# Feature-wise projections that hold weight blocks, a reordered last mixing, and a gather beside the experts

## The chip, the cores and the metric

The kernel runs on one core of a Trainium2 chip. The core has five engines that run their own instruction streams and wait for each other by semaphores: PE (TensorE, matrix products; PEld is its weight load), DVE (VectorE), ACT (ScalarE), POOL (GpSimd) and SP (SyncE, which here only issues transfers). The metric is the device time of one execution in microseconds, lower is better.

## What is computed

Two models stand one behind the other, on 256 tokens of width 1024, in float32. The first has two layers, each a mixer, a cross attention to a memory of 256 tokens, and a gated feed-forward net, each followed by a layer norm:

```python
x = layer_norm(ALPHA * x + mix(x), ...)                 # layer 0: mLSTM + neighbourhood attention; layer 1: differential attention
x = layer_norm(ALPHA * x + memory_cross_attention(x, mem, wq, wkv, wo), ...)
x = layer_norm(ALPHA * x + swiglu(x, w_gu, w_down), ...)  # hidden width 2816
```

The second has two layers on x and on a context xc of 256 tokens. Layer 1 needs of the context only its keys and values:

```python
h = rms_norm_2(x, n1) * (1 + sc1) + sh1                 # hc from xc likewise
a_b, a_c, a_h, b_v, b_g, c_q, c_k, c_v, d_q, d_k, d_v = split_proj(h @ w_in)
y = concat(short_conv(a), conformer_conv(b), window_attention(c), global_attention(d))  # keys of x and of xc
x = x + g1 * (y @ w_out)
h2 = rms_norm_2(x, n2) * (1 + sc2) + sh2
aff = softmax(h2 @ router)                              # 16 experts
gates, idx = top_k(aff.T, 32)                           # each expert takes 32 tokens
x = x + g2 * scatter(gates * (silu(xs @ w_gate) * (xs @ w_up)) @ w_down)   # xs = h2[idx]
```

## The kernel before

**Number format.** A matrix product of the dense layers is made of three products in the format fp32r: activations are split into a high and a low part (`xh`, `xl`), weights too (`wh`, `wl`), and `prod` adds xh·wh, xl·wh and xh·wl in one PSUM bank. Weights come from HBM in units of 1 MB (128 partitions x 2048 numbers) through a ring of buffers. `split` takes 1024 columns of a unit: ACT copies them to `wh`, DVE subtracts to get `wl`. There are two buffers of each.

**Dense layers.** In `dense_unit` (512 output features, tokens on the output's partitions) the activations are the stationary operand and the weights stream, 512 columns per matmul. Where a later step wants features on the partitions (the convolution's input, query and key of the neighbourhood attention, query and memory key of the cross attention, the hidden layer of the feed-forward net), the result is copied to `tk` or `ffh`, transposed on PE 128x128 at a time, and copied out of PSUM again (`acc_to_T`, and in `ffn` the four transposes of `gu`).

**Streams.** "M" is the main stream, x. "F" is a side stream: memory keys and the context, taken in pieces between the units of the main stream. A third runs the modulation of the second model. In the first block the feed-forward net interleaves `gu(j)` and `down(j)` for 11 blocks of 256 hidden features per layer. A scheduler orders each engine's instructions by priority when the program is built.

**Mixing of the second model.** `mixed` projects x: convolution a (`pa`), convolution b (`pb`), in layer 1 then the keys and values of xc (`kv_unit`), those of x, and last the queries (`query_unit`), all with norm and rotation in small DVE steps ended by transposes (`kd`, `tk`). `drip` puts single taps of the convolution (`cvo`, 128x256 multiply-adds on DVE) between other work, at rates given by `DRIP`. Attention (`attend`, with softmax weights `sx_e` that DVE scales by the reciprocal sum) and `out_proj` follow.

**Experts.** `begin` fetches the first units of the expert weights (2 in layer 0, 5 in layer 1). `route` takes x: transposes, router product, softmax (`aff`), 4 rounds of MAX8 and MATCH_REPLACE for the top 32, ranks (`code`). `gather` builds selection matrices `pm` and multiplies them with the normed x, itself split in `zh` and `zl` (the latter on POOL), into `XS`, 8 blocks of features. Then `expert_unit` goes through the units, 4 experts side by side on PE in layer 1 and 2 in layer 0. The ring of buffers is widened for this stage by `rings` that take over the space of tiles that are no longer used; `ORDER` says in which order, and `fetch` takes them cyclically, so a transfer waits for whoever held that space.

## Time and profile before

| | us |
|---|---|
| runs of the kernel before, median of 3 | 2389.7 (2388.44 to 2394.04) |
| the profiled execution | 2386.75 |
| its span in the trace | 2385.0 |
| outside the span | 1.75 |
| PE busy | 2080.6 (87%) |
| DVE busy | 1180.2 (49%) |
| ACT busy | 710.8 (30%) |

Times in the trace count from the start of the span. The stages are, by the lines and tiles that run in them: the first block up to 1035 us (feed-forward net of its first layer from 310 to 520), mixing of layer 0 from 1035 to 1225, out projection, routing and gather to about 1281, its experts to 1715, mixing and out projection of layer 1 to 1903, its routing and gather to 1930, its experts to 2366, and the last norm. Busy times of matmuls overlap each other's ends and are modelled; spacing from start to start is the better measure.

### The profile page before, as it was taken

What the parts mean: (1) busy time and instruction counts of PE and PEld (TensorE: products, weight loads), DVE (VectorE), ACT (ScalarE), POOL (GpSimd) and SP (SyncE); (2) the same over time, 40 slices, a digit from 0 to 9 for tenths busy, and PEclk for the clock granted to TensorE, in tenths of its full rate; (3) what the DMA queues carried; (4) which work ended last, traced back from release to release, by engine and by line L of the source; (5) the groups of instructions that cost most, each with busy time, mean ns of one, the idle gap of its engine ahead of it and who ended that gap; (6) DMA issues with size and microseconds to landing.
All of it is one profiled execution on the core that took longest, in us unless ns stands there. A gap on an engine that the chain in (4) does not pass through costs nothing.

```text
span 2385.0 us, 26936 instructions
## 1 busy us (share of the span) xinstructions
PE 2080.6 (87%) x10408; PEld 1243.2 (52%) x10408; DVE 1180.2 (49%) x2587; ACT 710.8 (30%) x1184; POOL 26.6 (1%) x20
## 2 busy tenths in 40 slices
PE   8999999999989999989898999988887976666665
PEld 5776777776767777767674333322265721010101
DVE  6586575557687697577973222111179621010001
ACT  5444444443455444444432000000053410000000
POOL 0001000000000000000010000000000000000000
PEclk9999999999999999999988999999998987777777
DMA  7745467666544464436437999999963299999997
GB/s 287 256 176 186 166 233 256 245 234 208 176 142 148 137 203 166 158 128 229 152 138 312 421 421 421 421 421 421 421 228 115 90 392 421 422 421 422 421 422 310
DMA packets 93584, 652.68 MB, mean 274 GB/s; under 512 B 10512, under 2 KB 11024, under 8 KB 15760
## 3 DMA queue, kind: packets, MB, share of 16 engines
q1 hardware_dynamic: 93456, 650.96, 70.7%
q8 instruction: 82, 1.34, 0.2%
q14 instruction: 46, 0.38, 0.0%
HBM read 649.87 MB, written 1.05 MB: 273 GB/s over the span
## 4 chain that ended last, share of the span: by engine, by line
PE 55%; DMA 30%; DVE 10%; ACT 3%; issue 1%; SPq 0%; POOL 0%; DVEq 0%; ACTq 0%; POOLq 0%
PE acc L108 33%; DMA ring<-in_w_up_dram 18%; PE ps L108 17%; DMA ring<-in_w_dn_dram 11%; PE ps L111 3%; DVE wl L124 3%; ACT wh L127 1%; DVE cvo L121 1%; PE acc L111 1%; DMA ring<-in_w_ada_dram 1%; ACT xh L127 0%; DVE z L121 0%; DVE rq_tM L118 0%; DMA ring<-in_w_even_dram 0%; DVE tk L124 0%
## 5 line engine op out<-in xcount | busy, mean ns | idle before, releaser
L124 DVE TENSOR_TENSOR wl<-ring,wh 128x1024 fp32r<-128x1024 f32 x346 | 422.9, 1224 | 243.1 <-ACT wh L127 237.3
L108 PE MATMUL acc<-ring,XS 128*64 128x512 f32 (+1 forms) x2048 | 409.2, 697 | 97.1 <-DMA ring<-in_w_up_dram 53.3
L127 ACT ACTIVATE wh<-ring 128x1024 fp32r<-128x1024 f32 x346 | 366.1, 1060 | 423.5 <-PE acc L108 284.9
L108 PEld LDWEIGHTS acc<-ring,XS 128*64 128x64 f32 (+1 forms) x2048 | 96.3, 129 | 395.6 <-issue 151.2
L108 PE MATMUL acc<-wh,xh 128*128 128x512 f32 (+1 forms) x736 | 289.3, 396 | 10.1 <-ACT xh L127 6.0
L108 PE MATMUL acc<-wl,xh 128*128 128x512 f32 (+1 forms) x736 | 286.6, 394 | 7.8 <-DVE wl L124 7.5
L108 PE MATMUL acc<-wh,xl 128*128 128x512 f32 (+1 forms) x736 | 289.2, 393 | 1.7 <-DVE xl L124 1.7
L121 DVE SCALAR_TENSOR_TENSOR mth<-mth,acc 128x512 f32<-128x512 f32 x24 | 16.5, 688 | 466.2 <-ACT mth L133 466.2
L108 PE MATMUL acc<-ring,hTm 128*64 128x512 f32 (+1 forms) x1024 | 206.4, 699 | 45.6 <-DMA ring<-in_w_dn_dram 44.9
L133 ACT ACTIVATE mth<-acc 128x512 f32<-128x512 f32 x24 | 14.3, 597 | 725.3 <-PE acc L108 725.3
L108 PEld LDWEIGHTS acc<-wh,xh 128*128 128x128 f32 x736 | 140.3, 192 | 42.1 <-ACT xh L127 7.9
L108 PEld LDWEIGHTS acc<-wl,xh 128*128 128x128 f32 x736 | 139.0, 190 | 43.1 <-DVE wl L124 14.0
L108 PEld LDWEIGHTS acc<-wh,xl 128*128 128x128 f32 x736 | 140.6, 191 | 33.0 <-DVE xl L124 5.5
L108 PEld LDWEIGHTS acc<-ring,hTm 128*64 128x64 f32 (+1 forms) x1024 | 47.9, 131 | 190.7 <-DMA ring<-in_w_dn_dram 100.3
L108 PE MATMUL ps<-wh,xh 128*128 128x512 f32 x368 | 145.6, 396 | 0.7 <-ACT wh L127 0.7
L108 PE MATMUL ps<-wh,xl 128*128 128x512 f32 x368 | 145.4, 395 | 0.0
L108 PE MATMUL ps<-wl,xh 128*128 128x512 f32 x368 | 145.0, 396 | 0.1
L124 DVE TENSOR_TENSOR my<-acc,gy 128x512 f32<-128x512 f32 x24 | 16.6, 692 | 227.6 <-PE acc L108 227.6
L108 PE MATMUL ps<-my,GT 128*128 128x512 f32 x160 | 82.3, 656 | 19.4 <-DVE my L124 19.4
L121 DVE SCALAR_TENSOR_TENSOR cvo<-pb,cols,cvo 128x256 f32<-128x256 f32 x180 | 82.0, 481 | 0.3
L108 PEld LDWEIGHTS ps<-wh,xh 128*128 128x128 f32 x368 | 69.2, 188 | 18.4 <-ACT wh L127 2.9
L108 PEld LDWEIGHTS ps<-wh,xl 128*128 128x128 f32 x368 | 69.3, 188 | 16.8 <-issue 3.5
(476 smaller groups left out, 2578.3 us busy)
## 6 DMA issues: line engine op xcount, KB each, us to landing
ring<-in_w_gate_dram SPq DMA_DIRECT2D x128, 1024.0 KB, 19.8
ring<-in_w_up_dram SPq DMA_DIRECT2D x128, 1024.0 KB, 19.8
ring<-in_w_dn_dram SPq DMA_DIRECT2D x128, 1024.0 KB, 19.8
ring<-in_w_ada_dram SPq DMA_DIRECT2D x48, 1024.0 KB, 4.9
ring<-in_w_gu_dram SPq DMA_DIRECT2D x44, 1024.0 KB, 4.9
ring<-in_w_in_dram SPq DMA_DIRECT2D x29, 1024.0 KB, 4.9
ring<-in_w_down_dram SPq DMA_DIRECT2D x22, 1024.0 KB, 4.9
ring<-in_w_memkv_dram SPq DMA_DIRECT2D x16, 1024.0 KB, 4.9
```

The source lines that it names most:

```text
L108: self.nc.tensor.matmul(out, lhsT=lhsT, rhs=rhs, start=start, stop=stop)
L111: self.nc.tensor.transpose(out, in_, self.ident)
L121: (eng or self.nc.vector).scalar_tensor_tensor(out, in0, s, in1, op0=op0, op1=op1)
L124: return (eng or self.nc.vector).tensor_tensor(out=out, in0=in0, in1=in1, op=op)
L127: self.nc.scalar.activation(out=out, in_=in_, func=AF.Copy, scale=scale)
L133: self.nc.scalar.activation(out=out, in_=in_, func=func, **kw)
```

## The change

**Feature-wise units.** A new `dense_T` makes 256 output features of a unit with the weight block stationary and the tokens moving: for a block of 128 inputs and 128 features one matmul of 512 columns (`wh`, with xh and xl side by side in one tile `xp`) and one of 256 columns (`wl`, with xh). On the side stream, where xh and xl are separate tiles, it is three matmuls of 256 columns. The bank's two halves are then added by `join`: an ACT copy of one and a DVE add of the other. It replaces product, copy, transposes and copy in `even_mixer`, the memory keys, the cross attention's queries and the feed-forward net. The host lays out the weights for it.

**Last mixing.** `mixed_last` takes layer 1 in another order: convolution b, queries' product, pre-norm of xc, norm and rotation of the queries, then keys and values of x and xc in one pass (`keys`, one load and split of the weights for both), convolution a, attention. Norm and rotation work on all heads at once. Taps drip at 3 and 4 in place of 2 and 6. In the wide attention of both layers every second scaling of `sx_e` goes to ACT.

**Routing and gather.** `route_start` and half of the transposes and of the router product of x (`route_part`) run within `out_proj`. The exponential of `aff` is issued ahead of the scaling of z and its split. `gather` yields after each of its 8 blocks, and the units already fetched are consumed between them. The ring's order changes.

```diff
+    def dense_T(self, X, w, u, accs=None):
+        accs = accs or [self.acc(), self.acc()]
+        s = self.load(w[u])
+        for q in range(2):
+            wh, wl = self.split(s[:, q * 1024:(q + 1) * 1024])
+            for kk in range(4):
+                k = q * 4 + kk
+                for c in range(2):
+                    ws = slice(kk * 256 + c * 128, kk * 256 + c * 128 + 128)
+                    o = accs[c][:, :256]
+                    if len(X) > 2:
+                        self.mm(accs[c].rearrange("p (a n) -> p a n", a=2), wh[:, ws], X[2][:, :, k], k == 0, False)
+                    else:
+                        self.mm(o, wh[:, ws], X[0][:, k], k == 0, False)
+                        self.mm(o, wh[:, ws], X[1][:, k], False, False)
+                    self.mm(o, wl[:, ws], X[0][:, k], False, k == 7)
...
+    def join(self, dst, acc, two, scale=1.0):
...
+        self.cp(dst, acc[:, 256:], scale)
+        if scale == 1.0:
+            self.tt(dst, acc[:, :256], dst, OP.add)
...
         def gu(j):
-            accs = self.dense_unit(X, self.a["w_gu"][l], j, accs=[self.ps(), self.ps()])
-            h = self.t([128, 2, 256], "ffh")
-            for t in range(2):
...
+            for c in range(2):
+                accs = self.dense_T(X, self.a["w_gu"][l], j * 2 + c, accs=[self.ps(), self.ps()])
+                g, u = self.t([128, 256], "ffg"), self.t([128, 256], "ffu")
+                self.join(g, accs[0], True)
+                self.join(u, accs[1], True)
                 th = self.t([128, 256], "th")
...
+                self.hl(H, c, 1, th[:, None], 0.5)
...
+    def mixed_last(self, x, xc):
+        l = 1
+        X = self.pre(x, l, 0)
+        pa = self.t([128, 2, 258], "pa")
+        self.proj_b(X, l, 0, pa)
+        accs = self.dense_unit(X, self.a["w_in"][l], 1)
...
+        Xc = self.pre(xc, l, 1)
+        self.queries(qs, l)
+        self.keys(X, Xc, l)
+        self.proj_a(X, l, pa)
+        self.begin(l)
...
+                    if self.wide and j:
+                        self.act(e[:, t], e[:, t], AF.Copy, scale=r[:, j, t:t + 1])
+                    else:
+                        self.ts(e[:, t], e[:, t], r[:, j, t:t + 1], None, OP.mult)
...
-        self.act(aff, aff, AF.Exp)
+        self.expd = self.act(aff, aff, AF.Exp)
+        with self.tc.issue_after(self.expd.ins):
+            for t in range(2):
+                self.act(z[:, t], x[:, t], AF.Copy, scale=rs[:, t:t + 1])
...
+        for k in self.gather(z, l, 0, XS):
+            while self.ahead and k > (steps[0][0] + 1) * (4 // ne) - 1:
+                self.expert_unit(*steps.pop(0), ne, part(0))
...
-ORDER = (0, 6, 2, 1, 5, 3, 4), (0, 8, 2, 1, 5, 4, 6, 7, 3)
+ORDER = ((0,), (3, 4), (6, 2, 1, 5)), ((0,), (3, 7), (8, 2, 1, 5, 4, 6))
...
-DRIP = ((2, 6), (1, 0))
+DRIP = ((2, 6), (1, 0), (3, 4))
```

How the instructions move is shown at three places. First, ACT in the feed-forward net of the first block, before: `th` is the tanh of the gate, `hTh` the high part of the transposed hidden block, `adae` belongs to the modulation.

```order
L127 ACTIVATE wh<-ring 128x1024 x2
L133 ACTIVATE th<-ps 128x256
L127 ACTIVATE wh<-ring 128x1024
L133 ACTIVATE th<-ps 128x256
L127 ACTIVATE wh<-ring 128x1024
L127 ACTIVATE hTh<-ps 128x512
```

The same engine and net in the changed kernel; `ffg` and `ffu` are the joined gate and up halves.

```order
L128 ACTIVATE wh<-ring 128x1024
L128 ACTIVATE ffg<-ps 128x256
L128 ACTIVATE wh<-ring 128x1024
L128 ACTIVATE ffu<-ps 128x256
L134 ACTIVATE th<-ffg 128x256
L128 ACTIVATE wh<-ring 128x1024
L128 ACTIVATE hTh<-th 128x256
```

For 128 hidden features there is now one `wh` ahead of each join's copy, and `th` waits for DVE's add in place of PE.

Second, PE in the mixing of layer 1, before, where the last projections of x end (`kd` are keys, `tk` queries, `KT` and `QT` the transposed ones, whose product opens attention).

```order
L108 MATMUL acc<-wl,xh 128x512
L111 MATMUL ps<-tabs,kd 128x128 x8
L111 MATMUL ps<-tabs,tk 128x128 x4
L108 MATMUL acc<-KT,QT 128x256
L111 MATMUL ps<-tabs,tk 128x128 x2
L108 MATMUL ps<-tabs,mods_3431 128x128 x3
L111 MATMUL ps<-tabs,tk 128x128 x2
```

In the changed kernel the queries' transposes stand within the product of the keys:

```order
L109 MATMUL acc<-wh,xh 128x512
L112 MATMUL ps<-tabs,tk 128x128 x4
L109 MATMUL acc<-wh,xl 128x512
L109 MATMUL acc<-wl,xh 128x512
L109 MATMUL acc<-wh,xh 128x512
```

and those of the keys, of both streams, stand behind the 48 matmuls of convolution a:

```order
L109 MATMUL acc<-wl,xh 128x512
L112 MATMUL ps<-tabs,kd 128x128 x16
L112 MATMUL ps<-tabs,cva 128x128 x4
L109 MATMUL ps<-tabs,mods_3722 128x128 x8
L109 MATMUL acc<-KT,QT 128x256 x4
```

So the queries' transposes have moved from the front of attention to a place with dense products ahead and behind; the keys' have stayed in front of attention.

Third, SP at the start of the experts of layer 1, before: each row is a unit of 1 MB, and what it waits for is who held its buffer.

```order
L1266 DMA ring_14291<-in_w_up_dram 128x2048 [waits DMAHW2_49,PE_49]
L1266 DMA ring_14315<-in_w_up_dram 128x2048 [waits DMAHW3_49]
L1266 DMA ring_14333<-in_w_gate_dram 128x2048 [waits DVE_49,DMAHW4_49,PE_49,Activation_49]
L1266 DMA ring_14339<-in_w_up_dram 128x2048 [waits DMAHW5_49,DVE_49,Pool_49]
L1266 DMA ring_14345<-in_w_gate_dram 128x2048 [waits DMAHW6_49,PE_49]
L1266 DMA ring_14351<-in_w_up_dram 128x2048 [waits DMAHW7_49,PE_49]
```

The same place in the changed kernel:

```order
L1425 DMA ring_14998<-in_w_up_dram 128x2048 [waits DMAHW0_49,PE_49]
L1425 DMA ring_15052<-in_w_gate_dram 128x2048 [waits DMAHW1_49,PE_49]
L1425 DMA ring_15058<-in_w_up_dram 128x2048 [waits DMAHW2_49,PE_49]
L1425 DMA ring_15022<-in_w_up_dram 128x2048 [waits DMAHW3_49]
L1425 DMA ring_15040<-in_w_gate_dram 128x2048 [waits DMAHW4_49,DVE_49,Activation_49]
L1425 DMA ring_15046<-in_w_up_dram 128x2048 [waits DMAHW5_49,Pool_49]
L1425 DMA ring_15064<-in_w_gate_dram 128x2048 [waits DMAHW6_49,PE_49]
```

Two units (15052 and 15058), which go into buffers that the first consumed units set free, have moved ahead of three (15022, 15040 and 15046) whose buffers come free with the routing.

## Rows read from the trace of the kernel before

**Rows 1.** The page, part 4: chain that ended last, share of the span

```profile
PE 55%; DMA 30%; DVE 10%; ACT 3%; issue 1%; SPq 0%; POOL 0%; DVEq 0%; ACTq 0%; POOLq 0%
```

**Rows 2.** Windows: length, busy PE, PEld, DVE, ACT, POOL (instructions), clock, DMA share, GB/s

```profile
0.00:1035.00 1035.00, 993.26 (x5107) 762.30 (x5108) 705.42 (x1359) 483.48 (x779) 11.36 (x12) 0.99 0.57 198
310.00:520.00 210.00, 209.17 (x1132) 160.20 (x1130) 121.15 (x183) 93.29 (x123) 0.00 (x0) 1.00 0.68 245
...
1312.00:1715.00 403.00, 367.32 (x1568) 123.36 (x1568) 79.72 (x156) 18.25 (x31) 0.00 (x0) 1.00 1.01 421
1715.00:1903.00 188.00, 155.97 (x763) 113.01 (x760) 141.28 (x391) 77.73 (x143) 0.00 (x0) 0.90 0.43 158
...
1930.00:2366.00 436.00, 297.21 (x1611) 54.04 (x1613) 31.61 (x62) 12.97 (x23) 0.00 (x0) 0.75 1.01 419
```

**Rows 3.** Timeline of PE, matmuls of 512 columns: start, duration

```profile
559.75 0.39 PE L108 MATMUL acc<-wh,xh 128*128 128x512 f32 x1
...
561.79 0.39 PE L108 MATMUL acc<-wh,xh 128*128 128x512 f32 x1
```

**Rows 4.** Timeline of PE, matmuls of 256 columns

```profile
823.68 0.28 PE L108 MATMUL acc<-wh,xl 128*128 128x256 f32 x1
...
825.59 0.28 PE L108 MATMUL acc<-wl,xh 128*128 128x256 f32 x1
```

**Rows 5.** Timeline of PE, four transposes in a row

```profile
332.59 0.60 PE L111 MATMUL acc<-tabs,tk 128*128 128x128 f32 x4
```

**Rows 6.** Waits of PE, first block: waited for, us in total, times, longest

```profile
PE acc L111 <- ACT tk L127: 1.8, 2, 0.9
```

**Rows 7.** Groups of ACT, 310 to 520 us: busy, mean ns, idle before, releaser

```profile
L127 ACT ACTIVATE wh<-ring 128x1024 fp32r<-128x1024 f32 x65 | 68.8, 1060 | 78.8 <-PE ps L108 55.2 <-PE acc L108 22.3
L133 ACT ACTIVATE th<-ps 128x256 f32<-128x256 f32 x22 | 8.2, 374 | 13.3 <-PE ps L108 13.3
```

**Rows 8.** Groups of DVE, 310 to 520 us

```profile
L124 DVE TENSOR_TENSOR wl<-ring,wh 128x1024 fp32r<-128x1024 f32 x66 | 80.8, 1226 | 69.9 <-ACT wh L127 69.8
L124 DVE TENSOR_TENSOR ffh<-th,ps 128x256 f32<-128x256 f32 x21 | 8.8, 420 | 0.6
```

**Rows 9.** Waits of PE, mixing of layer 1

```profile
PE ps L111 <- DVE tk L124: 9.8, 2, 9.5
...
PE ps L111 <- DVE kd L130: 3.2, 4, 1.0
PE ps L111 <- DVE cva L121: 2.7, 2, 2.1
PE acc L111 <- DVE sx_e L116: 2.6, 2, 2.1
```

**Rows 10.** Timeline of all engines, routing of layer 1 to its first units

```profile
1908.97 1.15 ACT L133 ACTIVATE z<-x,rq_zM 128x1024 f32<-128x1024 f32 x1 [2.86 <-DVE rq_zM L118]
...
1910.97 0.21 ACT L133 ACTIVATE aff<-aff 128x32 f32<-128x32 f32 x1
...
1911.14 4.64 POOL L124 TENSOR_TENSOR zl<-z,zh 128x1024 fp32r<-128x1024 f32 x2 [642.86 <-ACT zh L127]
...
1911.64 1.89 DVE L124 TENSOR_TENSOR aff<-aff,rt_rM 128x32 f32<-128x32 f32 x1
...
1915.80 0.33 SPq L1266 DMA_DIRECT2D ring<-in_w_up_dram  x1
...
1921.55 0.77 PE L108 MATMUL acc<-pm,zh 128*128 128x512 f32 x1 [1.10 <-DVE pm L124]
...
1930.43 0.33 SPq L1266 DMA_DIRECT2D ring<-in_w_gate_dram  x1
```

**Rows 11.** Timeline of all engines, routing of layer 0

```profile
1254.49 0.18 DVE L124 TENSOR_TENSOR aff<-rt_qM,rt_mM 128x32 f32<-128x32 f32 x1
...
1260.33 0.21 ACT L133 ACTIVATE aff<-aff 128x32 f32<-128x32 f32 x1
...
1271.12 0.77 PE L108 MATMUL acc<-pm,zh 128*128 128x512 f32 x1 [1.10 <-DVE pm L124]
```

More of the change, by code (lines that the diff above doesn't have):

```diff
@@ L1 @@
+import contextlib
 import itertools
@@ L420, in even_mixer @@
             nc.vector.memset(cpad[u][:, :, 258:260], 0.0)
[L421 to L425 removed]
+        w = a["w_evenT"]
+        for u in range(4):
+            accs = self.dense_T(X, w, u)
+            for c in range(2):
+                self.join(cpad[u // 2][:, (u % 2) * 2 + c, 2:258], accs[c], True)
         gT = self.t([16, 256], "gT")
@@ L652, in cross @@
         qT = self.big([128, 8, 256], "qk")
-        for u in range(2):
-            accs = self.dense_unit(X, self.a["w_memq"][l], u)
-            for t in range(2):
-                self.acc_to_T(accs[t], t, qT[:, u * 4:u * 4 + 4, t * 128:(t + 1) * 128])
+        for u in range(4):
+            accs = self.dense_T(X, self.a["w_memq"][l], u)
+            for c in range(2):
+                self.join(qT[:, u * 2 + c], accs[c], True)
         O = self.pair(8, "x")
@@ new lines, in mixed_last @@
+    def mixed_last(self, x, xc):
[4 more added lines that the diff above has]
+        accs = self.dense_unit(X, self.a["w_in"][l], 1)
+        qs = self.t([128, 2, 512], "qs")
+        for t in range(2):
+            self.cp(qs[:, t], accs[t])
+        Xc = self.pre(xc, l, 1)
[3 more added lines that the diff above has]
+        self.begin(l)
+        g = self.gate_rows(l, 2, 0)
+        self.wide = True
+        for _ in self.attend(l, 0):
+            pass
+        self.wide = False
+        self.convs(l, 0)
+        self.route_start(l, 0)
+        for _ in self.out_proj(l, 0, x, g):
+            pass
@@ L1209, in gather @@
         for t in range(2):
-            parts.append(self.split(z[:, t], self.nc.gpsimd, to and [v[:, t] for v in to]))
+            with (self.tc.issue_after(self.expd.ins) if r == 0 else contextlib.nullcontext()):
+                parts.append(self.split(z[:, t], self.nc.gpsimd, to and [v[:, t] for v in to]))
         for t in range(2):
@@ L1291, in moe, with part @@
         if nr > 1:
-            self.gather(self.zc, l, 1, XS)
-        self.gather(z, l, 0, XS)
+            for _ in self.gather(self.zc, l, 1, XS):
+                pass
+        first = [self.acc(), self.acc()]
+        steps = [(u, p) for u in range(2 * ne) for p in first]
+        def part(g):
+            return lambda k, j: XS[k][:, (g * ne + j) * M:(g * ne + j + 1) * M]
+        for k in self.gather(z, l, 0, XS):
+            while self.ahead and k > (steps[0][0] + 1) * (4 // ne) - 1:
+                self.expert_unit(*steps.pop(0), ne, part(0))
         nc8 = core[0][1]["C8"]
@@ L1302, in moe @@
             self.rings.append((p.__enter__(), n))
-        self.rings = [self.rings[i] for i in ORDER[l]]
-        a = self.a
+        early, late, rest = ([self.rings[i][0] for i in o for _ in range(self.rings[i][1])] for o in ORDER[l])
+        self.turns = itertools.chain(rest, itertools.cycle(early + late + rest))
         for g in range(ng):
@@ L1307, in moe @@
             for f in range(2):
-                pg, pu = self.acc(), self.acc()
-                for u in range(2 * ne):
-                    for p in (pg, pu):
-                        self.expert_unit(u, ne, p, lambda k, j: XS[k][:, (g * ne + j) * M:(g * ne + j + 1) * M])
+                pg, pu = first if g == 0 and f == 0 else (self.acc(), self.acc())
+                if g or f:
+                    steps = [(u, p) for u in range(2 * ne) for p in (pg, pu)]
+                for u, p in steps:
+                    self.expert_unit(u, p, ne, part(g))
                 th = self.t([128, 512], "mth")
```

231 lines of the change are left out of this document (156 added, 75 removed).

## The prediction

> **What bounds the kernel now.** I read the chain of what ended last first: PE holds 55% of it, transfers 30%, DVE 10% [rows 1]. That is an average over stages with different limits, so the windows come next [rows 2]. The first block fills 1035 us and PE is busy for 993 of them, in its first feed-forward net for 209.2 of 210. In both expert stages the DMA engines are busy all the time and move 420 GB/s, while PE keeps up at 1.2 GHz for much of the second one (granted clock 0.75). The mixing of layer 1 lies between: PE is busy for 156 of 188 us, DVE for 141, and neither fills it. So a us of PE work in the first block is worth a us; in the mixing only waits are; in the expert stages only the moment at which the stream of units starts and whether it pauses. The stages follow one another, so gains ahead of an expert stage shift all of it.
>
> **First block: the arithmetic on PE.** Matmuls of 512 columns start 2.04 us / 9 = 0.227 us apart [rows 3], those of 256 columns 1.91 / 16 = 0.119 [rows 4]. A matmul pair of `dense_T` costs 0.346; it does the work of one and a half 512-column products, 0.340. Counted in both programs, 960 pairs replace 1440 products on the main stream: 332.2 against 326.5, +5.7. On the side stream 128 triples of 256 columns replace 192 products: 45.8 against 43.5, +2.3. Away go 184 transposes (88 of `ffh`, 96 of `tk`) at about 0.11 us each, as four in a row span 0.60 of which a single one's latency is 0.27 [rows 5]: −20.2. Sum −12.2. There are two weight loads where there were one and a half; their cost lies inside the measured spacing at either width, since 256-column matmuls of the same kind already run at 0.119 with a load each. The waits of PE for `tk` [rows 6] go with the transposes: −1.8. I take −14.
>
> A page speaks against this edit: the Trainium skill, "TensorE: Matmul & The Clock Gate", section Back-to-back issue gap, gives a sustained spacing of 131 ns for 512 columns and 81 ns for 128, so fewer columns per load cost more per column. An estimate between its two figures is 98 ns for 256, and a pair would cost 229 ns against 196, +32 us over 960 pairs. The trace disagrees with both of its figures: 227 and 119 ns, a ratio of 1.9 [rows 3, 4].
>
> **First block: the joins.** Each of 60 main-stream units (44 in the nets, 8 in the even mixer, 8 in the cross attentions) has two joins: two ACT copies of 128x256 at 0.37 [rows 7] and two DVE adds at 0.42 [rows 8]. In exchange the copies around the transposes go. What hides them: between two `wh` copies ACT sits idle for PE's buffers, 78.8 us over 65 copies, 1.2 each [rows 7], and DVE idles 69.9 us ahead of 66 `wl` [rows 8]. The order on ACT puts one `wh` ahead of each join's copy, so half a unit's split (1.06 + 1.23 = 2.29) stands against 8 × 0.346 = 2.77 us of matmuls, and 0.48 is left: enough for one copy or add in front of it, not for both. I take nothing, with +10 as the other end (0.17 per unit), and −4 more if small stalls around the tails go. Bounds of the first block: −18 to −4.
>
> **Mixing of layer 0.** Half of the `sx_e` scalings leave DVE, each about half a us, in a stage bound mostly by PE: −1, from −4 to 0.
>
> **Routing of layer 0.** `aff` is ready at 1254.67, its exponential runs at 1260.33 behind `XS` copies and the scaling of z, and gather starts at 1271.12 [rows 11]. After, the exponential still stands behind four `XS` copies of the context's gather, but half of the router's product and transposes has gone into the out projection, and z and its split come later. If it issued at once, 5.7 + about 2 would be won; I take −4, from −8 to −1. Experts that start inside the gather only use PE time that the transfers leave.
>
> **Mixing of layer 1.** PE waits 9.8 us for the queries' `tk`, 3.2 for the keys' `kd`, 2.7 for convolution a, 2.6 for `sx_e` [rows 9]. After, the queries' norm and rotation run beside the keys' 96 matmuls (96 × 0.227 = 21.8 us): the 9.8 go. The keys' own chain of both streams now ends the projections: behind the last key matmul come copies, square, reduction, about ten small steps, eight multiplications, the rotation, 16 transposes and copies, with three `wl` (1.23 each) and a dozen taps between them on DVE, some 17 to 18 us from the chain of the same kind in the old trace. Beside it run 48 matmuls of convolution a, 10.9 us. So about 5 to 7 us of wait stay in front of attention. One pass for both streams saves four splits, −5 us of DVE, which is the engine behind most waits here, and two units of transfer. Sum of what goes: 9.8 + 3.2 + 2.7 + 2.6 + some 3 of smaller waits = 21; comes back: 6. I take −15; ends −20 (the chain hidden whole) and −5 (DVE behind in the keys too).
>
> **Routing and experts of layer 1.** The exponential at 1910.97 stood behind z (1.15) and one `zh` on ACT, and the next multiplication took 1.89 us while POOL made `zl` [rows 10]. Both delays go: 1.4 + 1.7. `zl` now runs later, beside the ranks, and may hold up a step there for as long again, so the ends are 1.4 and 5 with the router's half; I take gather 3 us earlier against the out projection. That DVE waits beside POOL agrees with the Trainium skill, "GPSIMD Engine Reference", section Key points: the two contend where DVE has two SBUF inputs.
> On SP the gain is lost again. Before, 18 units were issued by 1915.80, and the next at 1930.43 as the gather ended [rows 10]. After, two units that wait for the first consumed buffers stand ahead of three of the 18, so 15 are issued until the first expert units have run, which I put 4.3 us into the gather. Then 177 units remain in place of 174, at 436 us / 175 = 2.49 each [rows 2]: end = start + 4.3 + 2 + 441 = start + 447, before start + 444. Net 0, from −3 to +5.
>
> **Sum.** −14 −1 −4 −15 + 0 = −34 against the profiled 2386.75: 2353. That run lies 3 us below the median of those shown, 2389.7; from the median it is 2356. I say 2355. All good ends give −53, all bad ones −5; taken as independent the ends spread by about 12, so the likeliest case has its own range of 2340 to 2371.
>
> **Rivals.**
> *Joins eat the first block.* If the copies and adds delay each unit's split by 0.25 us, 15 us come back: 2371. For it: only 0.48 us of each 2.77 is free. Against: ACT's idle time above.
> *Slower.* The place is DVE in the feed-forward nets and mixers: if the in-order engine takes both adds (0.84) ahead of the next `wl` in every unit, PE, which has two weight buffers, stalls for all of it: 60 × 0.84 = +50, 2406. It decides from 34 / 60 = 0.57 us per unit on; slower by 0.3% needs 0.69. For it: DVE is the engine with the least room, 121 us of 210 plus 1.8 per 16 us. Against: the order alternates `wl` and adds.
> *The keys' chain replaces the queries'.* The wait before attention goes from 9.8 to some 15, the mixing wins 2, and the SP order costs its 5: −14 −1 −4 −2 + 5 = −16, 2374.
> *No change.* What PE saves is given back by waits of the same stage for transfers, whose share in the first block is 0.57 [rows 2], and the rest cancels: 2390. Against: a share of 0.57 leaves room.
>
> **Chances.** The forecast 0.64, joins eat it 0.13, keys' chain 0.10, no change 0.05, slower 0.08. Other runs of this kernel spread by 0.2%, so 0.3% (7 us) is about what can be told from no change. Faster takes the first three, 0.87; same 0.05; slower 0.08. The range takes in the likeliest case, most of the second and half of the third: 2338 to 2374.
>
> **What would show it.** In the profile after: no `ffh`, PE spacing 0.346 per pair and no wait of PE for `wl` above a few us in the first block, which ends near 1021; no 9.8 us wait for `tk` in layer 1, but one of 5 to 7 for `kd`; out projection of layer 1 done about 34 us earlier than 1903; gather 3 us closer to it; a pause of DMA in front of the first expert units of layer 1, and an end 447 behind the gather's start. Wrong it would be by waits for `wl` in every unit, or by a longer wait for `kd`.

## The result and the profile after

The changed kernel takes 2359.07 us (median of four runs, 2357.39 to 2359.95) against 2389.07 us beside it on the same chip: a ratio of 0.9884, 95% interval 0.9869 to 0.9899. The forecast was 2355, range 2338 to 2374. The profiled execution took 2359.95 us, its span is 2358.2.

The page of the changed kernel, busy times and the chain that ended last:

```profile
PE 2063.0 (87%) x10896; PEld 1262.1 (54%) x10896; DVE 1188.0 (50%) x2616; ACT 752.4 (32%) x1342; POOL 27.5 (1%) x20
...
PE 55%; DMA 30%; DVE 10%; ACT 3%; issue 1%; POOL 0%; SPq 0%; DVEq 0%; ACTq 0%; POOLq 0%
```

PE lost 18 us of busy time, ACT gained 42, and the chain is that of [rows 1]: averages over the span don't say where 27 us of it went. Three stretches of [rows 2] where they now lie, the third from the first product of gather to the last `hTm` matmul:

```profile
300.50:510.50 210.00, 208.63 (x1309) 168.85 (x1308) 135.70 (x234) 107.24 (x182) 0.00 (x0) 1.00 0.70 250
...
1697.00:1875.50 178.50, 155.19 (x778) 113.78 (x774) 129.03 (x334) 84.81 (x160) 0.00 (x0) 0.94 0.41 154
1891.40:2343.40 452.00, 307.48 (x1652) 60.47 (x1652) 35.58 (x70) 15.30 (x26) 0.00 (x0) 0.75 0.99 413
```

The feed-forward net is still full on PE, with more work on DVE (135.7 of 210, before 121.2) and ACT (107.2, before 93.3). The mixing of layer 1 has 12 us less DVE work. The last stretch of [rows 2] began 8.5 us into the gather. Cut like the line above, the experts of layer 1 in the kernel before read:

```profile
1921.50:2370.10 448.60, 308.37 (x1652) 61.02 (x1652) 35.60 (x70) 15.30 (x26) 0.00 (x0) 0.75 0.99 413
```

So the transfers' share is 0.99 in both: the kernel before had a pause of its own there, at the end of its gather (shares of 0.55 and 0.70 from 1925 to 1935).

For an account by stage I cut both timelines at the same instructions. A stage of the first block ends with the last statistics (`lnst`) of its layer norm; the mixing of the second model is cut at the first product KT·QT and at the last add into x; routing ends with the first product of gather, the experts with the last matmul on `hTm`. By this cut the first block of before ends at 1058.5 us, not at 1035.

| stage, us | before | after | difference | forecast |
|---|---|---|---|---|
| even mixer, first cross attention | 306.9 | 297.4 | −9.5 | |
| first feed-forward net | 229.6 | 226.9 | −2.7 | |
| odd mixer | 178.7 | 172.4 | −6.3 | |
| second cross attention | 93.9 | 98.6 | +4.7 | |
| second feed-forward net | 249.4 | 252.6 | +3.2 | |
| first block together | 1058.5 | 1047.9 | −10.6 | −14 |
| layer 0: mixing | 186.5 | 181.0 | −5.5 | −1 |
| layer 0: routing | 26.2 | 23.9 | −2.3 | −4 |
| layer 0: experts | 461.1 | 460.9 | −0.2 | 0 |
| layer 1: projections | 103.2 | 90.5 | −12.7 | |
| layer 1: attention, out projection | 67.9 | 71.4 | +3.5 | |
| layer 1: mixing together | 171.1 | 161.9 | −9.2 | −15 |
| layer 1: routing | 18.2 | 15.9 | −2.3 | −3 |
| layer 1: experts | 448.5 | 451.9 | +3.4 | +3 |
| sum | 2370.1 | 2343.4 | −26.7 | −34 |

**First block.** What PE waits for there, in us in total, times, longest:

```profile
PE acc L109 <- DVE qk L125: 4.5, 1, 4.5
PE acc L109 <- ACT wh L128: 3.8, 3, 2.3
PE acc L109 <- DVE wl L125: 2.6, 5, 0.8
...
PE acc L112 <- ACT cvb L128: 2.0, 1, 2.0
```

The waits for `tk` [rows 6] are gone. In their place stands one large wait, for a joined query tile `qk`, and small ones for the splits. The timeline around the large one, in the second cross attention, PE, DVE and ACT:

```profile
717.89 0.40 PE L109 MATMUL acc<-xp,wh 128*128 128x512 f32 x1
...
718.95 0.40 PE L109 MATMUL acc<-xp,wh 128*128 128x512 f32 x1
...
719.19 0.28 PE L109 MATMUL acc<-xp,wl 128*128 128x256 f32 x1
...
721.77 1.22 DVE L125 TENSOR_TENSOR x<-z,lnbc 128x1024 f32<-128x1024 f32 x1
...
723.02 0.66 ACT L128 ACTIVATE qk<-acc 128x256 f32<-128x256 f32 x2 [2.57 <-DVE x L125]
...
724.01 0.73 PE L109 MATMUL acc<-xp,wh 128*128 128x512 f32 x1 [4.54 <-DVE qk L125]
```

Three pairs of the new form take 1.06 us, 0.353 each, which the forecast put at 0.346. Then PE starts no matmul from 719.19 to 724.01. The join's copy on ACT was released by DVE's residual update, which reads `z`: the query tile takes the space of `z`, so the join waits for the last reader of `z`, and PE for the banks that the join holds.

In the second feed-forward net, 3.2 us longer, PE waits for `cvb` at its start, the context's convolution input. From one matmul's start to the next it is 2.40 us:

```profile
806.58 0.40 PE L109 MATMUL acc<-wl,xh 128*128 128x512 f32 x1
808.98 0.44 PE L112 MATMUL acc<-tabs,cvb 128*128 128x128 f32 x2 [2.00 <-ACT cvb L128]
```

The same gap is in the kernel before:

```profile
822.80 0.93 PE L111 MATMUL acc<-tabs,cvb 128*128 128x128 f32 x4 [2.00 <-ACT cvb L127]
```

What differs is the granted clock behind it. Windows of PE over the 8 us that begin with the gap (length, busy, clock, DMA share, GB/s), changed kernel, then the kernel before:

```profile
806.70:814.70 8.00, 5.95 (x36) 0.79 0.26 72
```

```profile
820.50:828.50 8.00, 5.95 (x43) 1.00 0.22 76
```

**Feed-forward nets.** Groups of ACT, then of DVE, in the stretch that answers to [rows 7, 8]:

```profile
L128 ACT ACTIVATE wh<-ring 128x1024 fp32r<-128x1024 f32 x65 | 68.7, 1059 | 52.3 <-PE ps L109 24.5 <-issue 14.0 <-PE acc L109 12.8
...
L128 ACT ACTIVATE ffg<-ps 128x256 f32<-128x256 f32 x22 | 8.5, 384 | 35.7 <-PE ps L109 35.7
```

```profile
L125 DVE TENSOR_TENSOR ffg<-ps,ffg 128x256 f32<-128x256 f32 x22 | 9.3, 424 | 16.2 <-ACT ffg L128 16.2
```

The joins cost what similar rows of before said (384 and 424 ns; 374 and 420 were taken). ACT still idles 52 us ahead of `wh`, most of it for PE's buffers: in the first net the joins fit.

**Mixing of layer 1.** Waits of PE:

```profile
PE acc L109 <- ACT xh L128: 4.6, 2, 3.2
PE ps L112 <- ACT kd L128: 3.9, 1, 3.9
PE acc L112 <- DVE sx_e L117: 2.5, 1, 2.5
```

The 9.8 us for the queries' `tk` [rows 9] are gone, and the keys take 3.9, less than the 5 to 7 forecast. New is the wait of 3.2 for `xh`: the out projection's first input comes from `cva`, convolution a. Its taps on DVE in the kernel before and in the changed one (min/median/max in ns, first and last start in us):

```profile
L121 DVE SCALAR_TENSOR_TENSOR cva<-pa,cols,cva x4: 480/480/482, 1771.7 to 1772.9; 128x256 f32<-128x256 f32 x4
```

```profile
L122 DVE SCALAR_TENSOR_TENSOR cva<-pa,cols,cva x4: 474/480/485, 1831.4 to 1835.5; 128x256 f32<-128x256 f32 x4
```

Before, they ran ahead of those of convolution b (`cvo`, from 1782.4 to 1855.3 us); now they run behind them (1748.9 to 1814.8). The change also moved the first multiplication of convolution a into the drip, behind the taps of b.

In attention and out projection together PE waits longer and is busy for less than before:

| attention, out projection of layer 1 | us | PE busy | PE idle | clock |
|---|---|---|---|---|
| kernel before | 67.9 | 62.1 | 5.8 | 0.90 |
| changed kernel | 71.4 | 60.4 | 10.9 | 0.95 |

**Routing and first units of layer 1**, timeline of ACT, DVE, POOL, PE and SP:

```profile
1877.38 1.28 SPq L1425 DMA_DIRECT2D ring<-in_w_up_dram  x2
...
1880.56 0.23 ACT L134 ACTIVATE aff<-aff 128x32 f32<-128x32 f32 x1 [3.46 <-DVE aff L125]
...
1880.70 2.17 ACT L134 ACTIVATE z<-x,rq_zM 128x1024 f32<-128x1024 f32 x2
...
1881.24 0.19 DVE L125 TENSOR_TENSOR aff<-aff,rt_rM 128x32 f32<-128x32 f32 x1
...
1883.89 4.64 POOL L125 TENSOR_TENSOR zl<-z,zh 128x1024 fp32r<-128x1024 f32 x2 [631.81 <-ACT zh L128]
...
1886.48 2.19 DVE L117 TENSOR_SCALAR tk<-tk 16x256 f32<-16x256 f32 x1
...
1891.44 0.76 PE L109 MATMUL acc<-pm,zh 128*128 128x512 f32 x1 [1.10 <-DVE pm L125]
...
1896.14 0.33 SPq L1425 DMA_DIRECT2D ring<-in_w_gate_dram  x1
```

The exponential no longer stands behind z, and the multiplication takes 0.19 where it took 1.89 [rows 10]. The delay beside POOL has moved to the ranks: a TENSOR_SCALAR of 16x256 takes 2.19 us. The same instruction in the kernel before, where POOL was done by then:

```profile
1918.50 0.28 DVE L116 TENSOR_SCALAR tk<-tk 16x256 f32<-16x256 f32 x1
```

SP issues nothing from 1878.7 until 1896.14, 4.7 us into the gather, and the transfers run dry (all engines, windows):

```profile
1890.00:1895.00 5.00, 3.90 (x10) 2.70 (x10) 3.11 (x8) 0.00 (x0) 0.00 (x0) 0.52 0.61 254
1895.00:1900.00 5.00, 5.00 (x38) 1.67 (x38) 0.81 (x1) 0.78 (x1) 0.00 (x0) 1.00 0.57 188
```

Shares of 0.61 and 0.57 over ten us are 4 us without transfers, about as long as the pause of before.

### The profile page after: what moved, and what is told of

Its sections match the earlier page's. It is cut to its first block, busy times and chain, and to the rows that moved or that the text cites. A ratio compares the mean times of both kernels' runs of the same rounds, so it can differ in the third digit from the quotient of the medians.

```text
span 2358.2 us, 28075 instructions
## 1 busy us (share of the span) xinstructions
PE 2063.0 (87%) x10896; PEld 1262.1 (54%) x10896; DVE 1188.0 (50%) x2616; ACT 752.4 (32%) x1342; POOL 27.5 (1%) x20
## 3 DMA queue, kind: packets, MB, share of 16 engines
q1 hardware_dynamic: 93168, 648.86, 71.2%
## 4 chain that ended last, share of the span: by engine, by line
PE 55%; DMA 30%; DVE 10%; ACT 3%; issue 1%; POOL 0%; SPq 0%; DVEq 0%; ACTq 0%; POOLq 0%
PE acc L109 35%; DMA ring<-in_w_up_dram 17%; PE ps L109 16%; DMA ring<-in_w_dn_dram 11%; PE ps L112 3%; DVE wl L125 2%; DVE cvo L122 1%; ACT wh L128 1%; PE acc L112 1%; DMA ring<-in_w_ada_dram 1%; ACT sx_e L134 1%; DMA nab<-in_rpb_dram 1%; ACT xp L128 0%; DVE tk L125 0%; ACT tov L134 0%
## 5 line engine op out<-in xcount | busy, mean ns | idle before, releaser
L109 PE MATMUL ps<-xp,wh 128*128 128x512 f32 x704 | 251.8, 399 | 3.5 <-ACT wh L128 1.9
L109 PE MATMUL ps<-xp,wl 128*128 128x256 f32 x704 | 198.8, 286 | 1.5 <-DVE wl L125 1.5
L109 PE MATMUL acc<-wh,xp 128*128 128x512 f32 x544 | 171.8, 397 | 2.8 <-ACT xp L128 1.6
L109 PEld LDWEIGHTS ps<-xp,wh 128*128 128x128 f32 x704 | 131.5, 188 | 38.1 <-ACT wh L128 5.1
L109 PEld LDWEIGHTS ps<-xp,wl 128*128 128x128 f32 x704 | 132.2, 189 | 11.4 <-issue 6.8
L109 PE MATMUL acc<-wh,xh 128*128 128x512 f32 (+1 forms) x336 | 131.1, 393 | 6.8 <-ACT xh L128 6.8
L109 PE MATMUL acc<-wl,xh 128*128 128x512 f32 (+1 forms) x336 | 129.0, 390 | 6.3 <-DVE wl L125 6.1
L109 PE MATMUL acc<-wh,xl 128*128 128x512 f32 (+1 forms) x336 | 130.7, 389 | 0.6 <-DVE xl L125 0.6
L109 PEld LDWEIGHTS acc<-wh,xp 128*128 128x128 f32 x544 | 101.8, 190 | 27.2 <-ACT wh L128 3.3
L109 PE MATMUL acc<-wl,xp 128*128 128x512 f32 x272 | 107.9, 403 | 0.6 <-DVE wl L125 0.5
```

What stands on the lines that cost most here:

```text
L109: self.nc.tensor.matmul(out, lhsT=lhsT, rhs=rhs, start=start, stop=stop)
```

## The experiments

All start from the changed kernel. Each ratio is against the kernel before on the same chip; the changed kernel's is 0.9884. Where a part of the kernel is concerned, the stage lengths of the table above are compared, each from one profiled execution. The interval of every single edit but one, the old order of the last mixing, overlaps that of the changed kernel, so whole runs alone don't tell them from it. Where an edit doesn't touch them the stages repeat within 1.7 us, with three exceptions: even mixer with first cross attention (294.1 to 297.4), odd mixer (171.2 to 175.8), and attention with out projection of layer 1 (71.2 to 75.1). The last two go with the granted clock: the odd mixer took 171.2 at 1.00 and 175.7 at 0.96; attention and out projection took 71.2 to 71.4 at 0.95 and 74.0 to 75.1 at 0.89 to 0.91, with the same waits of PE.

**Order on SP.** The two units that wait for consumed buffers go behind the three for the routing's buffers.

```diff
         t = next(self.turns).tile([128, UNIT], F32, name="ring")
-        self.nc.sync.dma_start(out=t, in_=next(self.units))
+        n = len(self.issued)
+        with (self.tc.issue_after(self.issued[17]) if ne == 4 and n in (18, 19) else contextlib.nullcontext()):
+            self.issued.append(self.nc.sync.dma_start(out=t, in_=next(self.units)).ins)
```

> The changed kernel, but in layer 1 the two units that wait for the first consumed buffers are issued behind the three whose buffers come free with the routing. Theory (the queue's order idles the transfers): in the changed kernel the DMA engines stand still for about 4 us of 1890 to 1900 us. With the three units ahead there is work for them until the first consumed buffer is free, so the experts end 4 us earlier against the gather's start (448 instead of 452 us from it to the last down product), and the kernel takes 2355 against 2359. Rival (the three buffers come free too late): the two units then queue behind a later wait, and it is the same or 1 to 3 us slower, 2359 to 2362.

2354.26 us (2351.19 to 2356.1), ratio 0.9868 [0.9851, 0.9886]. The experts of layer 1 take 446.1 instead of 451.9, and the transfers don't pause:

```profile
1890.00:1895.00 5.00, 5.00 (x26) 2.41 (x24) 0.81 (x1) 0.78 (x1) 0.00 (x0) 0.80 1.01 418
1895.00:1900.00 5.00, 5.00 (x34) 1.95 (x33) 0.81 (x1) 0.78 (x1) 0.00 (x0) 1.00 1.01 421
```

The order of two rows on SP costs 5.8 us. The theory had 4, and the rival's later wait didn't come.

**Gather alone.** Expert units wait for the whole gather.

```diff
         for k in self.gather(z, l, 0, XS):
-            while self.ahead and k > (steps[0][0] + 1) * (4 // ne) - 1:
-                self.expert_unit(*steps.pop(0), ne, part(0))
+            pass
```

> The changed kernel with gather run to its end before the first expert unit, in both layers; in this build the queue has the two units that wait for consumed buffers behind the three that come free with the routing. Theory (it is the queue's order that costs, and starting inside the gather is worth 3 us): from the gather's start to the last down product layer 1 takes 448 to 449 us as before the change, against 452 changed and 446 with the order mended; the kernel 2356. Rival (units inside the gather are what lengthens it, order apart): 444, 2352.

2360.6 us (2357.33 to 2362.83), ratio 0.9889 [0.9874, 0.9904]. The experts of layer 0 take 464.1 (+3.2). Those of layer 1 take 449.1, 2.8 less than in the changed kernel: in this build SP's rows stand in the good order. Against the run above, which has that order too, it is 3.0 more. So starting experts inside the gather is worth 3 us in each layer; in layer 1 the order that comes with it takes 5.8.

**Deferred updates.** The residual updates, spread over the splits after a layer norm, go in the order mult, mult, add, add, so that `z` is read out earlier. (The change itself had already made eight updates of 512 columns behind two empty places into four of 1024 behind one, which "The change" doesn't list.)

```diff
-        for t in range(2):
-            for j, (src, op) in enumerate(((z, OP.mult), (x, OP.add))):
+        for j, (src, op) in enumerate(((z, OP.mult), (x, OP.add))):
+            for t in range(2):
                 self.lazy.append(...)
```

> The changed kernel, but the postponed updates of x after each layer norm run in the order multiply, multiply, add, add over the two halves of the tokens, so that the tile z, whose space the cross attention's queries take, is read for the last time one weight split earlier. Theory (the join of the queries waits for that tile while it holds the accumulators): the 4.8 us gap of PE at 719 us of the changed kernel shrinks by about 3 us, 2356. Rival (the gap is the load of DVE itself at that place, with the context's work): it stays within 1 us of 4.8, 2359.

2357.32 us (2349.88 to 2358.85), ratio 0.9872 [0.9847, 0.9897]. PE's gap falls from 4.82 to 3.18, where about 3 less was expected, the second cross attention from 98.6 to 96.5: the mechanism holds, the size was half.

For the next run the updates also start one split earlier:

```diff
-        self.lazy += [None]
```

> The changed kernel with the deferred residual updates ordered mult, mult, add, add, as before, and with the empty place in front of them left out, so that each runs one split earlier. In the earlier version without that second step PE's gap behind the first query unit of the second cross attention was 3.18 us (4.82 in the changed kernel). Theory (the query tile shares the space of z and waits for the last reader of z): the gap shrinks by the length of one more split, 2.8 us, to below 1, and the second cross attention falls from 96.5 to 94 or less, the level of the kernel before. Rival (DVE is late there whatever the order, since updates and splits queue on it): the gap stays at 3 and only moves.

2350.74 us (2347.47 to 2359.56), ratio 0.9864 [0.984, 0.9888]. The gap is 1.40, above the 1 expected; the stage is 93.0, below the 93.9 of the kernel before. Of its 5.6 us 3.4 are the gap. The rest goes with the clock: its mean over the stage is 0.97 in the changed kernel, 0.98 in the run above and 1.00 here. PE around the gap:

```profile
716.08 0.28 PE L109 MATMUL acc<-xp,wl 128*128 128x256 f32 x1
717.48 0.50 PE L109 MATMUL acc<-xp,wh 128*128 128x512 f32 x1 [1.12 <-DVE qk L125]
```

In this run the second net takes 250.4, 2.2 less, with the wait for `cvb` as long as ever (2.39). Behind it the clock stays up:

```profile
799.00:807.00 8.00, 5.96 (x46) 1.00 0.30 92
```

PE's busy time in the net falls from 240.8 to 239.2: by that the clock behind the gap is worth 1.6 us.

**The gap at the second net.** The context's two copies `cvb` go ahead of the layer norm's later pieces on ACT.

```diff
             k = self.t([128, 512], "cvb")
-            self.cp(k, accs[t])
+            with (self.tc.high_priority(offset=200) if self.S == "F" else contextlib.nullcontext()):
+                self.cp(k, accs[t])
```

> The changed kernel with the two ACT copies of the context's convolution input (cvb) put ahead of the later pieces of the layer norm's transposed output, at the start of the second feed-forward net. In the changed kernel PE waits 2.40 us for them, and behind the gap the granted clock is 0.79 over 8 us; in the kernel before the same gap of 2.39 us leaves it at 1.00. Theory (the 3 us that the second net lost is that gap's clock, and not its products): without the gap the clock stays at 1.00 over 806 to 822, and the second net falls from 252.6 to 249 or 250, 2 to 3 us of the whole. Rival (the clock fell for another reason, or the net's own products are slower): 252 stays, or only the gap's 2 us or less come back with the clock still low. The late pieces come 1.2 us later on ACT; if PE then waits for them instead, that shows as a wait for xp.

2353.58 us (2351.3 to 2359.89), ratio 0.9868 [0.985, 0.9886]. The second net takes 249.5, 3.1 less, the level of before. The same stretch of PE in this run:

```profile
806.00:814.00 8.00, 7.45 (x54) 1.00 0.24 70
```

PE's idle time of 2.0 us in the gap shrinks to 0.5 and the clock stays up. The 3.1 holds both, half each: 1.5 of lowered clock (PE busy 240.8, now 239.3) and 1.6 of waiting, which the kernel before had too. The theory wanted 249 to 250 and has it. The rival's slower products are out: PE's busy time is below the 241.1 of the kernel before.

**Feed-forward nets in the old form**, weights streaming and hidden blocks transposed, all else as changed.

```diff
-            for c in range(2):
-                accs = self.dense_T(X, self.a["w_gu"][l], j * 2 + c, accs=[self.ps(), self.ps()])
...
+            accs = self.dense_unit(X, self.a["w_gu"][l], j, accs=[self.ps(), self.ps()])
```

> The changed kernel with the feed-forward nets as before (512 features a unit, tokens on the partitions, transposes). Theory from the two traces: the first net takes 208.4 us changed and 211.4 before, the second 226.4 and 224.7, so the feature-wise form is worth 1 us in all, 2360, since in the second net, beside the context's work on DVE, the joins give back what PE saves. Rival (the prediction's sum, 2.7 us saved in either net, and the second net is longer for another reason): 2364.

2362.04 us (2361.15 to 2364.22), ratio 0.9904 [0.9887, 0.992]. The first net takes 231.9 (+5.0), the second 252.5 (−0.1). That fits neither the theory (1 us in all) nor the rival (2.7 in either net). PE in both nets, by windows cut at the same places:

| net | kernel | us | PE busy | PE idle | clock |
|---|---|---|---|---|---|
| first | before | 229.6 | 228.8 | 0.8 | 1.00 |
| first | changed | 226.9 | 225.5 | 1.4 | 1.00 |
| first | old form put back | 231.9 | 228.3 | 3.6 | 1.00 |
| second | before | 249.4 | 241.1 | 8.3 | 1.00 |
| second | changed | 252.6 | 240.8 | 11.8 | 0.99 |
| second | old form put back | 252.5 | 243.1 | 9.4 | 0.99 |
| second | updates one split earlier | 250.4 | 239.2 | 11.2 | 1.00 |
| second | `cvb` ahead | 249.5 | 239.3 | 10.2 | 1.00 |

The new form saves PE 2.8 us of busy time in the first net and 2.3 in the second. In the first, the rest of the 5.0 comes with one wait in this run that the kernel before didn't have:

```profile
PE ps L112 <- DVE ffh L125: 2.6, 1, 2.6
```

In the second, PE waits 2.4 longer than with the old form, and the gain is gone. New among the waits of the changed kernel there are

```profile
PE ps L109 <- DVE ffg L125: 1.5, 2, 0.8
PE ps L109 <- ACT wh L128: 1.4, 3, 0.6
```

**Old order of the last mixing**, with its old rates of taps.

```diff
-        self.mixed_last(x, xc)
+        self.mixed(x, 1, xc)
...
-DRIP = ((2, 6), (1, 0), (3, 4))
+DRIP = ((2, 6), (1, 0), (2, 6))
```

> The changed kernel with the mixing of layer 1 in the order of before (keys of the context, keys of x, queries last, taps at 2 and 6), all else as changed. Theory (the new order is what layer 1 gained): from the last down product of layer 0 to x after the out projection it takes 171 us in place of 161.8, 2368. Rival (a good part of that came from the softmax scaling that ACT took over, which stays): 165 us, 2362.

2376.57 us (2371.72 to 2378.9), ratio 0.996 [0.9946, 0.9974]. The projections take 103.6, as before (103.2), attention and out projection 75.6. Together that is 179.2, where the theory had 171, the stage of before. The old wait is back:

```profile
PE ps L112 <- DVE tk L125: 9.8, 2, 9.5
PE acc L109 <- ACT xh L128: 6.2, 3, 3.2
```

The new order is worth 13 us in the projections. The 4 behind them are not shown to be its own: the clock there was 0.92 against 0.95, and with the new order the stage has taken up to 75.1. The wait of 3.2 for `xh` stands here too, and here as well convolution a's taps run behind those of b (from 1845.2 us): that points to their place on DVE, and not to the projection's place in the order. No run moves the first multiplication back alone, so it isn't shown.

**Taps faster**, six per softmax group instead of four.

```diff
-DRIP = ((2, 6), (1, 0), (3, 4))
+DRIP = ((2, 6), (1, 0), (3, 6))
```

> The changed kernel with one number altered: in the mixing of layer 1 six taps instead of four are dripped with each softmax group of the attention (three per split as before). The 68 taps then end two groups earlier. Theory (the out projection waits 3.2 us for xh because convolution a's taps, now the last ones, end too late): that wait goes, attention plus out projection of layer 1 falls from 71.4 us to 68 or 69, the whole kernel by 2 to 3 us. Rival (the taps only move the delay to the softmax steps on DVE, which is the busy engine there): the attention grows by what the out projection wins, the sum stays at 71 to 72, and the time within 1 us of the changed kernel's.

2354.78 us (2353.98 to 2356.51), ratio 0.987 [0.9855, 0.9884]. Waits of PE in the mixing of layer 1:

```profile
PE acc L109 <- ACT xh L128: 2.8, 2, 1.8
...
PE ps L112 <- DVE sx_e L117: 2.5, 2, 2.0
```

The wait for `xh` falls from 3.2 to 1.8, that of the softmax rises by 1.2 (2.5 for 1.3): attention and out projection take 70.7 instead of 71.4. That is nearer the rival, though the clock was lower too (0.93 against 0.95) and PE's idle time fell by 1.4. The rest of the lower time lies in other stages and is not explained by this edit.

**All scalings of `sx_e` on DVE.**

```diff
-                    if self.wide and j:
+                    if False:
```

> The changed kernel with all softmax scalings back on DVE in both layers. From the end of the last score product to x after the out projection, layer 1 takes 39 us before and 48 changed (and 48 with the old order of the mixing in the changed kernel); 3 us of that is the router's half, and PE waits 3 us longer for the high part of convolution a, which ACT copies. Theory (ACT is late because of the scalings it took over): this wait goes, layer 1 gains 4 us, layer 0 loses what it had gained, 4 of its 5.5 us; 2359, within 1 us. Rival (the wait comes from the taps of convolution a on DVE, which now start with their first product behind those of convolution b): the wait stays, both layers lose 1 to 4 us, 2362.

2366.0 us (2358.27 to 2366.82), ratio 0.9905 [0.9886, 0.9925]. From the last score product to the last add into x, layer 0 takes 60.3 instead of 54.2 (58.0 before); attention and out projection of layer 1 take 71.6 instead of 71.4. Waits of PE in that stretch of layer 0:

```profile
PE ps L112 <- DVE sx_e L117: 2.5, 1, 2.5
PE acc L112 <- DVE sx_e L117: 1.8, 2, 1.1
```

ACT's share is worth 6 us in layer 0. Over attention and out projection there, PE idles 9.9 us instead of 6.6 and the clock is 0.91 instead of 0.96, so about half of it is waiting. In layer 1 its worth isn't shown: without it PE idles 2.1 us less (the wait for `xh` falls from 3.2 to 2.6), at a clock of 0.91 instead of 0.95.

**Router half put back** behind the out projection.

```diff
-            if r == 0:
-                self.route_part(x, r, u)
             yield
...
-        if r:
-            self.route_start(l, r)
-            for u in range(2):
-                self.route_part(x, r, u)
+        if r:
+            self.route_start(l, r)
+        for u in range(2):
+            self.route_part(x, r, u)
```

> The changed kernel with the transposes and the router product of x all behind the out projection, as before; the early exponential and the gather stay. Theory (the half that moved is paid for in the out projection, which PE bounds): x after the out projection comes 3 us earlier in layer 1 and gather starts 3 us later against it, so nothing is won or lost there; in layer 0, where the router product ran at half clock, 2 us are lost: 2361. Rival (the prediction: the half is hidden): 2 to 4 us lost in each layer, 2365.

2366.09 us (2361.07 to 2366.92), ratio 0.9907 [0.9889, 0.9924]. Routing takes 27.9 in layer 0 (+4.0) and 20.5 in layer 1 (+4.6). Attention with out projection of layer 1 takes 72.3, not less, but at a clock of 0.88 against 0.95; "Gather alone", whose clock there was 0.89, took 75.1. So the clock hides what the half costs. The last 48 matmuls of the out projection ran at a granted clock of 1.00 in the changed kernel and in this run; the first and the last of them, changed kernel, then this run:

```profile
1859.70 0.39 PE L109 MATMUL acc<-wh,xh 128*128 128x512 f32 x1
...
1873.23 0.39 PE L109 MATMUL acc<-wl,xh 128*128 128x512 f32 x1
```

```profile
1865.43 0.39 PE L109 MATMUL acc<-wh,xh 128*128 128x512 f32 x1
...
1876.11 0.39 PE L109 MATMUL acc<-wl,xh 128*128 128x512 f32 x1
```

That is 13.5 us with the half between them and 10.7 without: it is paid for there with 2.9 us, as the theory said. In layer 1 the half is worth 4.6 − 2.9 = 1.7. In layer 0 the same matmuls take 11.8 and 10.8.

**Together.** Order and first step of the updates:

> The changed kernel with the mended order of the units of layer 1 and the postponed updates in the order multiply, multiply, add, add. Theory (two separate waits, in two stages): the gains add, 4 to 6 and 1 to 3 us, 2352. Rival (the second is run-to-run spread): 2354.

2348.04 us (2346.63 to 2350.48), ratio 0.9839 [0.9824, 0.9853]. The experts of layer 1 take 446.4 and the second cross attention 96.4, each as in its own run: the two add.

Order, both steps of the updates, `cvb` and taps:

> The changed kernel with four small edits together: the three routing buffers' units issued ahead of the two that wait for consumed buffers, the deferred residual updates reordered and one split earlier, the context's cvb copies put forward on ACT, and six taps per softmax group. By their own runs the experts of layer 1 should take 446 us instead of 451.9 (5.8), the second cross attention 93 instead of 98.6 (5.6), the second feed-forward net 248 to 249.5 instead of 252.6 (3 to 4), attention plus out projection of layer 1 70.7 instead of 71.4 (0.7). Theory (the four lie in stages that follow one another, so they add): 15 to 16 us below the changed kernel, 2343 or 2344. Rival (a part is counted twice, because the clock behind the cvb gap already recovered in the run with the updates one split earlier): the second net stays at 250 and the sum is 14 or less, 2346 or more.

2340.81 us (2337.37 to 2341.74), ratio 0.9803 [0.9786, 0.9821], 18 us below the changed kernel. By stages: second cross attention 93.1, second net 248.7, experts of layer 1 446.7, attention and out projection 70.8. They add: the four stages give 15.2, and the sum of all stages is 17.0 less than in the changed kernel (2326.4 against 2343.4).

## Why the prediction was right, and where its terms were off

The forecast of 2355 missed by 4 us; the likeliest case was the one that happened, with errors in its terms that partly cancel. By its steps:

**Arithmetic of the first block.** Right, as far as it was taken apart. Pairs run at 0.353 (0.346 taken), the transposes are gone. For the two nets the sum gives 704 × 0.006 = +4 and 88 × 0.11 = −9.7, or −5.5; PE's busy time falls by 2.8 and 2.3 against the old form. Even mixer and first cross attention win 9.5, but no run puts the old form back there alone. That the block came out at −10.6, near −14, is in part luck: the odd mixer, which the forecast left alone, won 6.3 and paid for most of two losses that no term had (4.7 and 3.2). Of the 6.3, 4.2 is an idle stretch in the trace of before that has no releaser and is in none of the changed kernels' traces (waits of PE, 560 to 580 us):

```profile
PE acc L108 <- issue: 4.2, 1, 4.2
```

The other 2.1 are the size of the odd mixer's own spread with the clock. What removed the stretch stays open.

**Joins.** "I take nothing" holds in the first net. In the second, waits for joins and splits take back the 2.3 us that PE saves. It failed outright at one place, the second cross attention: not by the time of copies and adds, but by the space of the tile that they write. The joined `qk` waits for the last reader of `z`, 4.8 us, and with `z` read earlier 3.4 of them are gone and 5.6 from the stage, the clock that comes back with them included. Before, the query went to `tk` first, and to `qk` only behind its transposes; I had counted the join's length and not what it has to wait for.

**Second net.** +3.2 that no term had. By the table above, PE idles 3.5 us longer than before, 2.4 of it by the new form; the other 1.1 is not explained. PE's busy time is as before, 240.8 and 241.1: the products save 1.9 where the clock stays at 1.00 (239.2), and the lowered clock behind the first gap, which was there before, takes 1.6 back.

**Mixing of layer 0.** −1 was too small: −5.5. The scalings on ACT are worth 6 there by the run without them, half of it waits of PE and half a higher clock. I had counted their half a us each on DVE and neither of these.

**Routing of both layers.** −2.3 and −2.3 against −4 and −3. The router's half takes 4.0 and 4.6 out of routing, but it is not hidden: the out projection pays 1 and 2.9 for it. In layer 1 the wait of the exponential was smaller than the 1.4 in the forecast: in the trace of before `aff` was ready at 1910.21 and the exponential ran at 1910.97. What came back is the delay beside POOL, named as a possibility: 2.19 us now on a step of the ranks.

**Mixing of layer 1.** −9.2 against −15. The projections did what was said: the 9.8 went, 3.9 came for `kd`. The mis-sized part lies behind them, where the forecast had a gain and +3.5 was measured. I put the router's half into the out projection at no cost, and it costs 2.9. I let the waits for convolution a (2.7) and `sx_e` (2.6) go; `sx_e` still has 2.5 and 1.3, and convolution a, with its taps now behind those of b, makes the out projection wait 3.2. Faster taps take 1.8 off the waits for `xh` and add 1.2 to those of the softmax. PE's idle time rose by 5.1 in all; part of that was made up by a clock of 0.95 in place of 0.90, which no term had.

**Experts of layer 1.** The mechanism and its size are right: +3.4 against +3, SP's next issue 4.7 us into the gather (4.3 forecast). Two parts of opposite sign make it up: the order costs 5.8, the experts inside the gather give back 3.

By the stages the sum is −27 in place of −34, nearer than its terms. The mixing of layer 1 fell short by 6, the first block by 3 and routing by 2; the mixing of layer 0 gave 4 more.

## What to carry to other kernels

When an operation writes to another tile than the one it replaces, look up who read that space last: a join whose copy takes 0.4 us and whose add takes 0.4 cost 4.8 here through its tile. When a change orders transfers by hand, compare the first moment at which each can issue: in an in-order queue, two that wait for work still to come shut out three that could go. And work moved into another stage has to be priced there: the router's half left routing by 4.6 us and lengthened the out projection, which PE fills, by 2.9. Compare stages at the same granted clock before calling such a price nothing.

## What was not expected of the hardware

The granted clock behind a gap does not follow from the gap's length alone. The same idle time of 2.0 us of PE at the start of the second net, with the same 5.95 or 5.96 us of busy PE in the 8 us that begin with it, left the clock at 1.00 in the kernel before and in the run with the updates one split earlier, and was followed by 0.79 in the changed kernel, 82 us behind another gap of 4.8 us. In the ten traces of changed kernels that have this gap and in which the clock had also fallen behind the earlier gap, at the query tile, it fell here too; in the two where it had not fallen there, it stayed up here. That is a coincidence in twelve traces and no cause shown: what decides it was not found.

POOL's subtraction held up a DVE instruction with a single tensor as input: a TENSOR_SCALAR of 16x256 took 2.19 us while POOL made `zl`, until POOL was done, and 0.28 in the kernel before without it. Not every instruction waits: in the same 4.64 us MAX8 and MATCH_REPLACE8 on 16x256 took 0.42 and 0.40, as in the kernel before. The trace of before had such a row already, in the routing of the context: a TENSOR_SCALAR of 16x256 took 2.52 us at 1236.92, beside POOL.
